# Expert weight tiles stored as 8192-byte rows, and a tile ring laid out anew in 4096 more SBUF columns

## The chip, the core and the metric

The kernel runs on one core of one Trainium2 chip. The metric is device time in microseconds (us) of one launch, the median over several runs. Everything is float32; the weights lie in HBM and are loaded in each launch.

## The reference

Two layers (DEPTH = 2) over 256 context tokens and 256 latent tokens of width 1024. Each layer runs three token mixers side by side (S5 state space, latent attention, windowed attention), merges them, and then runs a mixture of experts; only the latent stream is returned, so the second layer leaves the context out of its last steps. What matters here is the second half of a layer, the experts:

```python
N_EXPERTS = 16; EXPERT_FF = 1024; CAPACITY_FACTOR = 2

def expert_choice_ffn(h, lp):
    B, N, D = h.shape
    cap = CAPACITY_FACTOR * N // N_EXPERTS                 # 32 tokens for each expert
    aff = softmax(h @ lp['w_router'], axis=-1)
    g, idx = lax.top_k(aff.swapaxes(1, 2), cap)
    xs = jax.vmap(lambda hb, ib: hb[ib])(h, idx)
    a = jnp.einsum('becd,edf->becf', xs, lp['w_gate'])     # w_gate, w_up, w_down: (2, 16, 1024, 1024)
    u = jnp.einsum('becd,edf->becf', xs, lp['w_up'])
    y = jnp.einsum('becf,efd->becd', jax.nn.silu(a) * u, lp['w_down']) * g[..., None]
    return scatter_add(idx, y)

def trunk_layer(xc, xl, ...):
    hc, hl = modulate(xc, ...), modulate(xl, ...)          # adaLN
    yc, yl = token_mixer(hc, hl, ...)                      # three branches, gates, w_out
    xl = layer_norm(ALPHA * xl + mod_l[2] * yl, ln1)
    fl = expert_choice_ffn(modulate(xl, ...), lp)
    xl = layer_norm(ALPHA * xl + mod_l[5] * fl, ln2)       # and the same for xc in layer 0
    return xc, xl
```

All 16 experts of both layers are used whatever the routing does: 3 matrices of 4 MB for each expert, 201 MB for each layer.

## The kernel before

`Net.build` (near L1690) runs the layers in order. `layer` (L1735) has a mixer part, in which S5, attention and gates are interleaved by hand (`fill`, `tick`), an output projection (`out_proj`, L1352), the first layer norm with the router (`out_norm`, `scores`, `choose`), and `moe` (L1569). A scheduler places the instructions of all engines after that; only those marked with `keep_in_program_order` stay where they were written. All loads are issued by SyncE (SP) on one queue.

**The tile ring.** `expert_ring` (L1395) cuts each expert into 12 tiles of 1 MB: a tile is two blocks of 128 rows of one matrix (`kh` and `kh + 1`), on 128 partitions with 2048 columns each. So there are 192 tiles for each layer. Its `grow` adds buffers to the ring as the rest of the layer frees them, `issue` loads the next tiles into the buffers that are ready, and `weight(i)` hands tile i to TensorE and gives the buffers of the tiles before it back to the ring. A buffer carries a number: from that tile on it is not reused (192: reused to the end; 0: used once). The load of a tile is one line:

```python
i = self.load(ap, self.ins[nm][l, e].rearrange("(k p) (c n) -> p k c n", p=128, n=NF)[:, kh:kh + 2])
```

In HBM the matrix lies row by row, so a partition gets two runs of 1024 floats, 4096 bytes each, from rows 128 apart. `hold=True` in `grow` leaves issuing to `feed`, which `out_proj` calls at every second of its eight steps, so that weights of the projection and expert tiles share the queue.

**Where the buffers lie.** One SBUF tile of 23360 columns, `arena`, holds most data, at places written out by hand in `PLACES` (L1868): `E`, `F1` to `F5` are ring buffers of 2048 columns in the arena, `lngb1` the rows of the first layer norm, `m2` the adaLN gate, `mht` and `mxn` router data, `eth`, `eht`, `m5`, `rwt`, `cm`, `ys` the experts' small buffers. Other ring buffers are blocks that the mixer has done with (`big`, `extra`, `h`), half of `xs` once, and `more` in layer 1. In layer 0 the ring has 21 buffers, five of them used once; in layer 1 it has 22, two of them used once.

**What consumes a tile.** In `moe` expert e takes 8 tiles for gate and up (TensorE, output `sc`), then SiLU on ACT and VectorE (L1616 to L1618), four transposes (`tp`), and 4 tiles for down (output `mm`). After every fourth expert the results are scattered; the tokens of the first four experts are gathered at the start and those of the later groups after experts 3, 6 and 8 (`F`, `ad`). In layer 0 each token tile has 64 rows (both streams), in layer 1 it has 32. In experts 9 to 15 of layer 0 the S5 setup of layer 1 (`s5_setup`, L511) is woven in: its loads `s5_prm`, `s5_dk`, `s5_b`, `s5_c` (shown as `in_s_prm` and so on), its arithmetic on VectorE (L550), and transposes on TensorE.

Of the kernel before, what the change touches and what calls it, by code (L numbers as in the profile page):

```python
# [14 lines left out]
D = 1024  # L15
KT = 8
DEPTH = 2
N_EXP = 16
# [139 lines left out]
class Net:  # L158
# [1236 lines left out]
    def expert_ring(self, l):  # L1395

        NF = 512 if l == 0 else 256
        view = lambda t: t.rearrange("p (k c n) -> p k c n", k=2, n=NF)
        ready, once, tiles, at = [], {"single": 0}, {}, [0, 0]

        def grow(*where, blocks=(), single=(), hold=False):


            for w, until in where:
                name = f"F{len(once)}"
                once[name] = until
                ready.append((name, view(self.buf(name, 2048, at=w))))
            for block, until in blocks:
                for i in range(0, int(block.shape[1]), 2048):
                    name = f"block{len(once)}"  # L1410
                    once[name] = until
                    ready.append((name, view(block[:, i:i + 2048])))
            for block in single:
                ready.append(("single", view(block)))
            if not hold:
                issue(len(ready))

        def issue(n, behind=False):

            for _ in range(min(n, len(ready), 192 - at[0])):  # L1420
                e, r = divmod(at[0], 12)
                a, kh = self.part_of(e, r)
                nm = ("w_gate", "w_up", "w_down")[a]
                name, ap = tiles[at[0]] = ready.pop(0)
                i = self.load(ap, self.ins[nm][l, e].rearrange("(k p) (c n) -> p k c n", p=128, n=NF)[:, kh:kh + 2])
                if behind:
                    self.tc.keep_in_program_order(i)
                at[0] += 1

        def weight(i):  # L1430
            while at[1] < i:
                name, ap = tiles.pop(at[1])
                at[1] += 1
                if at[0] < once.get(name, 192):
                    ready.append((name, ap))
                elif name in self.A.live:
                    self.free(name)
            issue(len(ready))
            return tiles[i][1]

        return weight, grow, lambda: issue(1, True)

    def part_of(self, e, r):
# [246 lines left out]
    def build(self, layers=(0, 1), stop=None):  # L1690
        tc, nc = self.tc, self.nc
        self.dbg_out = {}
        self.fillq, self.adaq, self.debt, self.ada_debt = [], [], 0.0, 0.0
        with tc.tile_pool(name="main", bufs=1) as main, \
                tc.tile_pool(name="small", bufs=1) as small, \
                tc.tile_pool(name="ps", bufs=1, space=PSUM) as psum:
            self.small, self.psum, self.main = small, psum, main
            self.sc = main.tile([128, KT * 32], F32, name="silu_c")
            self.modT = [main.tile([128, 6, KT, 2], F32, name=f"modT{i}") for i in range(2)]
            k1 = main.tile([128, 4], F32, name="k1")  # L1700
            self.mhalf, self.econst, self.hpi, self.ones1 = [k1[:, i:i + 1] for i in range(4)]
            for ap, val in ((self.mhalf, -0.5), (self.econst, math.e), (self.hpi, math.pi / 2), (self.ones1, 1.0)):
                nc.vector.memset(ap, val)
            self.const = main.tile([128, NCONST], F32, name="const")
            arena = main.tile([128, self.ARENA_COLS], F32, name="arena")
            self.A = Arena(arena, self.ARENA_COLS)
            self.adaR, self.OH, self.ah, self.cd, self.back, self.norm, self.rw, self.rrow = {}, {}, {}, {}, {}, {}, {}, {}
            self.adarow = [self.buf(f"ada{i}", 512, low=True) for i in range(2)]
            x = {t: self.buf(f"x{t}", D, low=True) for t in range(4)}
            self.ada_start()  # L1710
            self.load(self.const[:, 0:128], self.ins["const"][:, 0:128])
            self.S, self.early, self.stats, self.T, self.feed = {}, [], {}, {}, lambda: None
            self.setup = self.s5_setup(layers[0], self.S, 16)
            next(self.setup)
            self.stg = self.rot("stg", 1024, 4, True)
            hb = [self.block(f"h{i}", F32) for i in range(2)]
            bufs = [hb[i // 2][:, 2048 * (i % 2):2048 * (i % 2) + 2048] for i in range(4)]
            bufs += [self.block(f"extra{i}", F32)[:, 0:2048] for i in range(2)] + [self.buf("wada", 2048, True)]
            for k, _ in enumerate(self.ada_group(layers[0], 0, bufs)):
                if k == 4:  # L1720
                    for t in range(4):
                        self.load(x[t], self.xin(t))
                if k in (7, 8):
                    kc = len(self.early)
                    self.early.append(self.wload(self.w_in(layers[0], 0, 512)[:, 2 * kc:2 * kc + 2], 2, 512))
            self.free("wada")
            for l in layers:
                self.layer(l, x, 1 if l == 0 and 1 in layers else None)
            for t in (2, 3):
                self.load(self.out[0, (t - 2) * 128:(t - 1) * 128], x[t])  # L1730
# [4 lines left out]
    def layer(self, l, x, nxt):  # L1735
        tc, nc = self.tc, self.nc
# [3 lines left out]
        with tc.tile_pool(name=f"parts{l}", bufs=1, reuse_waits="tile") as self.R:  # L1740
# [16 lines left out]
            mT = self.buf("mT", KT * N, True, 12416 if full else None).rearrange("p (k n) -> p k n", k=KT)  # L1757
# [25 lines left out]
            T = self.T = self.PLACES[l]  # L1783
# [23 lines left out]
            else:  # L1807
                mb = self.block("big0", F32R)
                m = self.out_split(mT, [mb[:, 0:2048], mb[:, 2048:4096]])
            self.free("mT")  # L1810
            self.slots = self.buf("slots", 256, at=T["slots"])
            gb = self.ln_rows(l, 1)
            wr = self.buf("wr", 128, True, T["wr"]).rearrange("p (k e) -> p k e", k=KT)
# [7 lines left out]
            m2 = {}  # L1821
# [15 lines left out]
        with tc.tile_pool(name=f"late{l}", bufs=1, reuse_waits="tile") as pool:  # L1837
# [10 lines left out]
            for s in ((1, 0) if full else (1,)):  # L1848
                self.out_norm(l, pts[s], x, s, gb)
                if s == 2 - NS:  # L1850
# [9 lines left out]
            self.T = {}  # L1860
            tts = (0, 1, 2, 3) if full else (2, 3)
            self.free(*[n for n in self.A.live if n[0] in "EF"])
            self.finish(l, x, pts, nxt is not None)

    ARENA_COLS = 23360
    BLOCKS = dict(h0=4096, h1=4096, big0=4096, big1=4096, big2=2048, extra0=2064, extra1=2064)

    PLACES = [dict(E=((21312, 172), (19264, 172)), raff=9216, wr=9344, rls=9472, rw=9600, rrow=10112, slots=10240, mxn=(10496, 11520, 12544, 13568),  # L1868
                   oh=14592, lngb1=15104, m2=17152, mht=8192, eth=4096, eht=4608, m5=5120, rwt=5632, ys=6144, cm=5888,
                   F1=((4096, 0), (6144, 0)), F2=((17152, 160),), F3=((15104, 160),), F4=((0, 0), (2048, 0)),  # L1870
                   F5=((8192, 192),)),
              dict(E0=(7168, 192), E1=(13312, 0), E2=((15360, 192), (9216, 192), (11264, 192)),
                   raff=19200, wr=18944, rls=19072, rw=19264, rrow=19520, slots=18688, mxn=(17408, 6144), oh=18432,
                   lngb1=2048, m2=3072, mht=20288, eth=13312, eht=13568, m5=13824, rwt=14080, ys=14336, cm=18944,
                   F1=((21312, 192),), F2=((4096, 192),), F3=((2048, 192),), F4=((0, 0),), F5=((19264, 192),))]
    NWC = 4

    FEED_OUT = [[0, 1] * 4, [0, 1] * 4]
# [4 lines left out]
def _prepare(inputs):  # L1883
    f = lambda n: np.ascontiguousarray(np.asarray(inputs[n]))
    a = {}
    for n in ("x", "ctx", "w_in", "s5_w_glu", "win_sink", "w_branch", "w_out", "ln1_g", "ln1_b",
              "ln2_g", "ln2_b", "w_router", "w_gate", "w_up", "w_down"):
        a[n] = f(n)
    c, cc = f("c").reshape(D), f("c_ctx").reshape(D)
    a["c2"] = np.stack([cc.reshape(KT, 128), c.reshape(KT, 128)], -1).transpose(1, 0, 2).reshape(128, KT * 2)  # L1890

# [33 lines left out]
def _program(arrays, dbg=None, layers=(0, 1), **tckw):  # L1925
    tckw.setdefault("schedule_with_timeline_sim", True)
    import concourse.bacc as bacc
    import concourse.tile as tile

    nc = bacc.Bacc("TRN2", target_bir_lowering=False, num_devices=1)  # L1930
    ins = {n: nc.dram_tensor("in_" + n, v.shape, mybir.dt.from_np(v.dtype), kind="ExternalInput").ap()
           for n, v in arrays.items()}
    out = nc.dram_tensor("out_0", (1, 256, D), F32, kind="ExternalOutput").ap()
    with tile.TileContext(nc, **tckw) as tc:
        net = Net(tc, ins, out, dbg)
        net.build(layers)
    return nc, net
# [9 lines left out]
```

## Time and profile before

| what | value |
|---|---|
| time, median of 3 runs | 2122.13 us (2119.47 to 2123.6) |
| the profiled execution | 2119.83 us, span 2118.1 us |
| TensorE busy | 1805.4 us (85%) |
| VectorE, ACT, GpSimd busy | 1046.0, 610.9, 452.7 us |
| DMA | 544.20 MB, mean 257 GB/s |
| TensorE clock granted, mean | 0.912 |

The span runs from the first to the last instruction; the execution's own time is 1.7 us longer. The profile cuts the span into 40 slices of about 53 us. TensorE's busy time is modelled from its pipeline, so a high share does not say that it sets the pace; the waits and the chain of work that ended last say that. The DMA figures of a slice tell how near the 16 DMA engines are to what they can move.

### The profile page before, as it was taken

The numbers are of one execution on the slowest core, as the hardware profiler recorded it, in microseconds if no ns is written. First come the engines' busy times: TensorE is split into PE (matmuls) and PEld (weight loads), VectorE is DVE, ScalarE is ACT, GpSimd is POOL, SyncE is SP. The second block draws the span as 40 slices with busy tenths as digits, with TensorE's granted clock in tenths as the row PEclk, the third lists the DMA queues.
The fourth block names the chain that finished last, engine by engine and source line by source line (L and its number), as shares of the span: only waits on it lengthen the run. The fifth ranks groups of instructions, "written<-read, shape, count | busy, mean of one in ns | idle before, by whom it ended". The sixth has DMA issues, their size and how long they took to land. (4 is left out here: it accounts for less than half of the span.)

```text
span 2118.1 us, 31735 instructions
## 1 busy us (share of the span) xinstructions
PE 1805.4 (85%) x12425; PEld 1121.1 (53%) x12425; DVE 1046.0 (49%) x2431; ACT 610.9 (29%) x1353; POOL 452.7 (21%) x590
## 2 busy tenths in 40 slices
PE   5999899999998799999799889789997856676765
PEld 3876666677776534434233278787875422232222
DVE  6767666656538622322563357977757311110102
ACT  2344253444434320101110155654553100000000
POOL 5735320011135100001442025630114000000000
PEclk8899999999999799999999989999998987676766
DMA  8236745522247699999999623341467799999996
GB/s 310 63 125 218 249 135 167 162 70 70 61 131 288 249 358 409 409 409 404 405 402 395 270 65 98 86 145 50 114 243 272 313 408 409 409 409 409 409 409 270
DMA packets 222165, 544.20 MB, mean 257 GB/s; under 512 B 18624, under 2 KB 101696, under 8 KB 221120
## 3 DMA queue, kind: packets, MB, share of 16 engines
q1 hardware_dynamic: 222016, 542.18, 69.4%
q8 instruction: 98, 1.61, 0.3%
q14 instruction: 51, 0.42, 0.1%
HBM read 541.09 MB, written 1.05 MB: 256 GB/s over the span
## 5 line engine op out<-in xcount | busy, mean ns | idle before, releaser
L243 PE MATMUL F<-h,wc 128*128 128x256 f32 (+1 forms) x1200 | 237.8, 350 | 10.9 <-ACT arena L1295 8.9
L404 ACT ACTIVATE wc<-arena 128x512 fp32r<-128x512 f32 (+2 forms) x280 | 169.9, 619 | 223.1 <-DMA arena<-in_w_in 44.7
L407 DVE TENSOR_TENSOR wc<-arena,wc 128x512 fp32r<-128x512 f32 (+2 forms) x205 | 164.0, 812 | 115.0 <-ACT wc L404 114.2
L243 PE MATMUL sc<-arena,xs 128*32 128x256 f32 (+1 forms) x1176 | 166.5, 524 | 59.9 <-DMA arena<-in_w_up 35.0
L243 PEld LDWEIGHTS F<-h,wc 128*128 128x128 f32 x1200 | 189.0, 196 | 42.2 <-ACT arena L1295 9.9
L246 PE MATMUL tp<-const,arena 128*128 128x128 f32 (+2 forms) x819 | 137.1, 293 | 70.1 <-DVE arena L1618 14.3
L1641 DVE TENSOR_TENSOR arena<-mm,arena 32x512 f32<-32x512 f32 (+1 forms) x128 | 70.9, 554 | 217.1 <-PE mm L243 215.5
L407 POOL TENSOR_TENSOR wc<-arena,wc 128x512 fp32r<-128x512 f32 (+2 forms) x75 | 98.0, 1306 | 369.2 <-ACT wc L404 296.1
L243 PE MATMUL mm<-arena 128*32 128x256 f32 (+5 forms) x1076 | 164.4, 461 | 13.5 <-DMA arena<-in_w_down 6.9
L246 PEld LDWEIGHTS tp<-const,arena 128*128 128x128 f32 (+2 forms) x819 | 97.2, 147 | 130.8 <-issue 40.9
L238 ACT ACTIVATE arena<-tp 128x512 f32<-128x512 f32 (+3 forms) x142 | 61.9, 462 | 331.4 <-PE tp L246 313.5
L260 POOL TENSOR_TENSOR lnq<-lnq,k 128x1 f32<-128x1 f32 x22 | 17.6, 802 | 594.4 <-DVE lnq L307 556.7
L243 PEld LDWEIGHTS sc<-arena,xs 128*32 128x32 f32 (+1 forms) x1176 | 53.6, 132 | 151.7 <-issue 75.0
L243 PE MATMUL sc<-h,xs 128*32 128x256 f32 (+1 forms) x760 | 116.1, 537 | 13.3 <-DMA h<-in_w_up 8.2
L243 PEld LDWEIGHTS mm<-arena 128*64 128x64 f32 (+2 forms) x1076 | 69.6, 137 | 85.6 <-issue 43.0
L1616 ACT ACTIVATE arena<-sc 128x512 f32<-128x512 f32 (+1 forms) x32 | 15.7, 491 | 336.0 <-PE sc L243 336.0
L243 PE MATMUL sc<-big,xs 128*32 128x256 f32 (+1 forms) x688 | 91.6, 522 | 22.7 <-DMA big<-in_w_gate 12.6
L1618 DVE TENSOR_TENSOR arena<-arena,sc 128x512 f32<-128x512 f32 (+1 forms) x32 | 17.7, 553 | 181.6 <-PE sc L243 181.4
L1617 DVE SCALAR_TENSOR_TENSOR arena<-arena,sc 128x512 f32<-128x512 f32 (+1 forms) x32 | 17.7, 555 | 172.1 <-ACT arena L1616 172.0
L243 PE MATMUL mm<-wc,h 128*128 128x512 f32 (+2 forms) x288 | 81.3, 408 | 9.5 <-ACT h L496 5.3
L243 PE MATMUL F<-extra,wc 128*128 128x256 f32 (+1 forms) x432 | 85.2, 341 | 3.2 <-DVE arena L1330 2.9
L550 DVE TENSOR_TENSOR arena<-arena 128x64 f32<-128x64 f32 (+2 forms) x300 | 81.0, 316 | 12.8 <-POOL arena L553 6.1
(344 smaller groups left out, 3210.4 us busy)
## 6 DMA issues: line engine op xcount, KB each, us to landing
arena<-in_w_gate SPq DMA_DIRECT2D x53, 1024.0 KB, 18.1
arena<-in_w_down SPq DMA_DIRECT2D x48, 1024.0 KB, 18.2
arena<-in_w_up SPq DMA_DIRECT2D x44, 1024.0 KB, 18.5
arena<-in_w_ada SPq DMA_DIRECT2D x82, 512.0 KB, 4.9
h<-in_w_down SPq DMA_DIRECT2D x41, 1024.0 KB, 18.2
h<-in_w_up SPq DMA_DIRECT2D x37, 1024.0 KB, 15.9
arena<-in_w_in SPq DMA_DIRECT2D x66, 512.0 KB, 4.0
big<-in_w_gate SPq DMA_DIRECT2D x30, 1024.0 KB, 18.5
```

Source lines behind the costliest of these rows:

```text
L238: self.nc.scalar.activation(out, in_, AF.Copy)
L243: return self.nc.tensor.matmul(out, lhsT, rhs, start=start, stop=stop, skip_group_check=True)
L246: self.nc.tensor.transpose(out, in_, self.c("idn")[:n, :n])
L260: self.nc.gpsimd.tensor_tensor(out, in_, e.to_broadcast(list(in_.shape)), op=OP.pow)
L404: nc.scalar.activation(hi, src, AF.Copy)
L407: eng.tensor_tensor(lo, src, hi.bitcast(F32), op=OP.subtract)
L550: tt = lambda o, a, b, op: v.tensor_tensor(o, a, b, op=op)
L1616: nc.scalar.activation(th, gu[0][:, :NF], AF.Tanh, scale=0.5)
L1617: v.scalar_tensor_tensor(th, th, 1.0, gu[0][:, :NF], op0=OP.add, op1=OP.mult)
L1618: v.tensor_tensor(th, th, gu[1][:, :NF], op=OP.mult)
L1641: v.tensor_tensor(YS[n][o:o + 32, c * NF:(c + 1) * NF], yp[r:r + 32, :NF], m5[r:r + 32], op=OP.mult)
```

## The change

Three things are changed. The host stores each tile as one contiguous block of 128 rows of 8192 bytes, in the order in which SBUF takes them, and the load reads one row for each partition. The program is built with a descriptor scratch of 64 bytes, and the arena gets 4096 columns (16 KB on each partition) more. `PLACES` is written anew: the new columns, called `late` until the projection, take the norm rows, the gate and the experts' small buffers, and ring buffers take what these leave.

```diff
-                i = self.load(ap, self.ins[nm][l, e].rearrange("(k p) (c n) -> p k c n", p=128, n=NF)[:, kh:kh + 2])
+                i = self.load(ap, self.ins[nm][l, e, kh // 2].rearrange("p (k c n) -> p k c n", k=2, n=NF))
...
+            self.buf("late", 4096, at=self.LATE)
             self.adarow = [self.buf(f"ada{i}", 512, low=True) for i in range(2)]
...
-            self.free("mT")
+            self.free("mT", "late")
+            grow(*T["E3"], hold=True)
             self.slots = self.buf("slots", 256, at=T["slots"])
...
             self.free(*[n for n in self.A.live if n[0] in "EF"])
+            self.buf("late", 4096, at=self.LATE)
             self.finish(l, x, pts, nxt is not None)
 
-    ARENA_COLS = 23360
+    ARENA_COLS = 27456
+    LATE = 23360
...
-    PLACES = [dict(E=((21312, 172), (19264, 172)), raff=9216, wr=9344, rls=9472, rw=9600, rrow=10112, slots=10240, mxn=(10496, 11520, 12544, 13568),
-                   oh=14592, lngb1=15104, m2=17152, mht=8192, eth=4096, eht=4608, m5=5120, rwt=5632, ys=6144, cm=5888,
-                   F1=((4096, 0), (6144, 0)), F2=((17152, 160),), F3=((15104, 160),), F4=((0, 0), (2048, 0)),
...
+    PLACES = [dict(E=((21312, 172), (19264, 172), (17152, 160)), E3=((15104, 160),), raff=9216, wr=9344, rls=9472, rw=9600,
+                   rrow=10112, slots=10240, mxn=(10496, 11520, 12544, 13568), oh=14592, lngb1=23360, m2=25408, mht=8192,
+                   eth=23360, eht=23872, m5=24384, rwt=24896, cm=25152, ys=25408,
+                   F1=((4096, 192), (6144, 192)), F2=(), F3=(), F4=((0, 0), (2048, 0)), F5=((8192, 192),)),
...
-                   lngb1=2048, m2=3072, mht=20288, eth=13312, eht=13568, m5=13824, rwt=14080, ys=14336, cm=18944,
-                   F1=((21312, 192),), F2=((4096, 192),), F3=((2048, 192),), F4=((0, 0),), F5=((19264, 192),))]
+              dict(E0=(7168, 192), E1=(13312, 192), E2=((15360, 192), (9216, 192), (11264, 192)),
+                   E3=((2048, 192), (5120, 192)),
...
+                   lngb1=23360, m2=24384, mht=20288, eth=23360, eht=23616, m5=23872, rwt=24128, ys=24384, cm=18944,
+                   F1=((21312, 192),), F2=((25408, 192),), F3=(), F4=((0, 0),), F5=((19264, 192),))]
...
+    for n in ("w_gate", "w_up", "w_down"):
+        a[n] = f(n).reshape(DEPTH, N_EXP, 4, 2, 128, D).swapaxes(3, 4).reshape(DEPTH, N_EXP, 4, 128, 2 * D)
...
-    nc = bacc.Bacc("TRN2", target_bir_lowering=False, num_devices=1)
+    nc = bacc.Bacc("TRN2", target_bir_lowering=False, num_devices=1, dynamic_dma_scratch_size=64)
```

The ring of layer 0 keeps 21 buffers, of which three instead of five are used once; that of layer 1 has 23, one used once.

The scheduler then gives another order. Three places on SP follow; a row is a load, out<-in and its shape, and x2 means two in a row. The first is the output projection of layer 0, before:

```order
L229 DMA arena<-in_w_gate 128x2x1024
L229 DMA arena<-in_w_out 128x1024 x2
L229 DMA arena<-in_w_up 128x2x1024
L229 DMA extra_5691<-in_w_down 128x2x1024
L229 DMA arena<-in_ctx 128x1024
L229 DMA extra_5690<-in_w_down 128x2x1024
L229 DMA arena<-in_x 128x1024
L229 DMA arena<-in_ln_g 128x1024
L229 DMA arena<-in_ln_b 128x1024
```

and with the change:

```order
L229 DMA arena<-in_w_gate 128x2048
L229 DMA arena<-in_w_out 128x1024 x2
L229 DMA arena<-in_w_up 128x2048
L229 DMA extra_5692<-in_w_gate 128x2048
L229 DMA arena<-in_ctx 128x1024
L229 DMA extra_5691<-in_w_down 128x2048
L229 DMA arena<-in_x 128x1024
L229 DMA arena<-in_w_down 128x2048
```

A tile's load has become one run of 2048 floats for each partition instead of two of 1024, and the rows of the layer norm (`in_ln_g`, `in_ln_b`) are gone from here: a tile stands in their place. They now stand near the start of the program, behind the first small loads and ahead of `w_in`:

```order
L229 DMA bglu<-in_s_bg 128x4
L229 DMA mlagn<-in_mla_gain 128x5
L229 DMA sink<-in_win_sink 128x8
L229 DMA arena<-in_ln_g 128x1024
L229 DMA arena<-in_ln_b 128x1024
L229 DMA arena<-in_w_in 128x2x512 x2
```

Those of layer 1 have moved likewise, from its output projection to ahead of the first loads of its mixer. The second place is in the experts of layer 0, where the loads of layer 1's S5 setup begin, before:

```order
L229 DMA arena<-in_s_b 128x2x64
L229 DMA arena<-in_w_up 128x2x1024
L229 DMA extra_5690<-in_w_up 128x2x1024
L229 DMA arena<-in_s_c 128x2x64 x2
L229 DMA extra_5691<-in_w_up 128x2x1024
L229 DMA h_5696<-in_w_down 128x2x1024
L229 DMA arena<-in_s_prm 128x96
L229 DMA arena<-in_s_dk 128x4
```

and with the change:

```order
L229 DMA arena<-in_s_b 128x2x64
L229 DMA arena<-in_w_up 128x2048
L229 DMA extra_5691<-in_w_down 128x2048
L229 DMA arena<-in_s_c 128x2x64 x2
L229 DMA arena<-in_s_prm 128x96
L229 DMA arena<-in_s_dk 128x4
```

The parameters `in_s_prm`, with which the setup's arithmetic begins, have two tiles instead of four between them and the first `in_s_b`. On TensorE the setup's transposes and small products stand where they stood: three transposes, four expert matmuls, one transpose and three more, as here with the change.

```order
L246 MATMUL tp_7253<-const,arena 128x128 x3
L243 MATMUL sc_7211<-arena,xs 64x512 x4
L246 MATMUL tp_7253<-const,arena 128x128
L246 MATMUL tp_7262<-const,arena 128x128 x3
L243 MATMUL sc_7211<-arena,xs 64x512 x4
```

The same five steps before the change had the same kinds and counts, and the fifth read its tile from `extra`.

## Rows read from the trace of the kernel before

**Rows 1.** Page, 40 slices: busy tenths of TensorE and DMA, and GB/s.
```profile
PE   5999899999998799999799889789997856676765
DMA  8236745522247699999999623341467799999996
GB/s 310 63 125 218 249 135 167 162 70 70 61 131 288 249 358 409 409 409 404 405 402 395 270 65 98 86 145 50 114 243 272 313 408 409 409 409 409 409 409 270
```
**Rows 2.** Chain that ended last, in order of time: start us, us, what.
```profile
1674.85 15.73 DMA big<-in_w_up
1690.58 20.38 DMA arena<-in_w_down
...
2079.79 19.09 DMA arena<-in_w_down
2098.87 0.04 issue
```
**Rows 3.** TensorE's waits, 1675 to 2100 us: waited for, us in total, times, longest.
```profile
PE sc L243 <- DMA arena<-in_w_up: 33.5, 18, 11.6
PE sc L243 <- DMA arena<-in_w_gate: 23.3, 18, 2.9
```
**Rows 4.** Windows: stretch, length, busy PE, PEld, DVE, ACT, POOL; clock, DMA share, GB/s.
```profile
800.00:950.00 150.00, 144.66 (x686) 58.06 (x682) 43.69 (x87) 13.56 (x28) 0.00 (x0) 1.00 1.03 409
1000.00:1150.00 150.00, 128.18 (x680) 45.92 (x682) 89.78 (x346) 23.26 (x83) 66.92 (x200) 0.97 1.03 400
1750.00:2050.00 300.00, 201.45 (x1980) 75.42 (x1972) 34.64 (x82) 10.24 (x26) 0.00 (x0) 0.72 1.03 409
```
**Rows 5.** Windows of the start, in which tiles of w_ada are loaded.
```profile
6.00:17.00 11.00, 7.08 (x60) 2.48 (x64) 4.13 (x30) 0.35 (x2) 8.77 (x2) 1.00 1.01 425
23.00:27.00 4.00, 0.29 (x4) 0.20 (x8) 4.00 (x11) 0.00 (x0) 1.62 (x2) 0.50 1.02 424
5.00:16.00 11.00, 6.08 (x52) 2.08 (x56) 3.17 (x22) 0.35 (x2) 9.77 (x2) 1.00 1.00 417
```
**Rows 6.** Page: DMA packets, and the instruction queues' among them.
```profile
DMA packets 222165, 544.20 MB, mean 257 GB/s; under 512 B 18624, under 2 KB 101696, under 8 KB 221120
...
q8 instruction: 98, 1.61, 0.3%
q14 instruction: 51, 0.42, 0.1%
```
**Rows 7.** TensorE's waits in the experts of layer 0, 740 to 1200 us.
```profile
PE tp L246 <- DVE arena L550: 10.3, 3, 6.1
...
PE sc L243 <- DMA arena<-in_w_up: 1.5, 1, 1.5
PE sc L243 <- DMA h<-in_w_up: 1.3, 2, 0.7
...
PE sc L243 <- DMA arena<-in_w_gate: 0.8, 2, 0.6
```
**Rows 8.** VectorE by line, 800 to 1200 us: count, busy us, mean ns, idle before.
```profile
L550 DVE TENSOR_TENSOR arena<-arena 128x64 f32<-128x64 f32 (+1 forms) x219 | 43.9, 248 | 3.9 <-POOL arena L553 1.4 <-DVE arena L550 0.2
...
L550 DVE TENSOR_TENSOR big<-arena 128x64 f32<-128x64 f32 x32 | 8.7, 271 | 0.9
```
**Rows 9.** Windows: behind the first loads, and the start of layer 1.
```profile
40.00:50.00 10.00, 9.82 (x37) 8.75 (x37) 10.00 (x17) 4.56 (x10) 8.00 (x10) 0.77 0.58 205
1200.00:1250.00 50.00, 36.40 (x127) 24.39 (x124) 36.70 (x80) 27.16 (x54) 13.48 (x13) 0.80 0.15 44
```
**Rows 10.** Page, DMA issues: count, KB each, median us from issue to landing.
```profile
arena<-in_w_gate SPq DMA_DIRECT2D x53, 1024.0 KB, 18.1
```

More of the change, by code (lines that the diff above doesn't have):

```diff
@@ L1862, in layer @@
             self.free(*[n for n in self.A.live if n[0] in "EF"])
+            self.buf("late", 4096, at=self.LATE)
             self.finish(l, x, pts, nxt is not None)
-    ARENA_COLS = 23360
+    ARENA_COLS = 27456
+    LATE = 23360
     BLOCKS = dict(h0=4096, h1=4096, big0=4096, big1=4096, big2=2048, extra0=2064, extra1=2064)
-    PLACES = [dict(E=((21312, 172), (19264, 172)), raff=9216, wr=9344, rls=9472, rw=9600, rrow=10112, slots=10240, mxn=(10496, 11520, 12544, 13568),
-                   oh=14592, lngb1=15104, m2=17152, mht=8192, eth=4096, eht=4608, m5=5120, rwt=5632, ys=6144, cm=5888,
-                   F1=((4096, 0), (6144, 0)), F2=((17152, 160),), F3=((15104, 160),), F4=((0, 0), (2048, 0)),
-                   F5=((8192, 192),)),
-              dict(E0=(7168, 192), E1=(13312, 0), E2=((15360, 192), (9216, 192), (11264, 192)),
-                   raff=19200, wr=18944, rls=19072, rw=19264, rrow=19520, slots=18688, mxn=(17408, 6144), oh=18432,
-                   lngb1=2048, m2=3072, mht=20288, eth=13312, eht=13568, m5=13824, rwt=14080, ys=14336, cm=18944,
-                   F1=((21312, 192),), F2=((4096, 192),), F3=((2048, 192),), F4=((0, 0),), F5=((19264, 192),))]
+    PLACES = [dict(E=((21312, 172), (19264, 172), (17152, 160)), E3=((15104, 160),), raff=9216, wr=9344, rls=9472, rw=9600,
[4 more added lines that the diff above has]
+                   E3=((2048, 192), (5120, 192)),
+                   raff=19200, wr=18944, rls=19072, rw=19264, rrow=19520, slots=18688, mxn=(17408, 4096), oh=18432,
+                   lngb1=23360, m2=24384, mht=20288, eth=23360, eht=23616, m5=23872, rwt=24128, ys=24384, cm=18944,
+                   F1=((21312, 192),), F2=((25408, 192),), F3=(), F4=((0, 0),), F5=((19264, 192),))]
     NWC = 4
@@ L1886, in _prepare @@
     for n in ("x", "ctx", "w_in", "s5_w_glu", "win_sink", "w_branch", "w_out", "ln1_g", "ln1_b",
-              "ln2_g", "ln2_b", "w_router", "w_gate", "w_up", "w_down"):
+              "ln2_g", "ln2_b", "w_router"):
         a[n] = f(n)
+    for n in ("w_gate", "w_up", "w_down"):
+        a[n] = f(n).reshape(DEPTH, N_EXP, 4, 2, 128, D).swapaxes(3, 4).reshape(DEPTH, N_EXP, 4, 128, 2 * D)
     c, cc = f("c").reshape(D), f("c_ctx").reshape(D)
```

## The prediction

> **What bounds the kernel now.** I read the page's slices first, then the chain of waits, then TensorE's waits in the two expert stages, then windows of the stages. The slices show two plateaus on which DMA moves about 409 GB/s: slices 16 to 22 (experts of layer 0) and 33 to 39 (experts of layer 1) [rows 1]. The mixers between them leave the queue half empty. A plateau of DMA is a bound only where somebody waits for it, and here the two stages differ.
>
> In layer 1 the chain runs through loads of expert tiles from 1674.85 us to the last landing at 2098.87 us, and then 19 us of scatter and norm [rows 2]. TensorE waits for tiles of gate and up throughout, 33.5 and 23.3 us in the two largest groups alone [rows 3]; it is busy in 201 of 300 us, while the queue never leaves 409 GB/s [rows 4]. So each 1 MB tile (1.0486 MB by its bytes) costs 1.0486 / 0.409 = 2.564 us, and the stage ends when the last tile is in.
>
> In layer 0 DMA is as full, but TensorE is nearly full as well: 144.7 of 150 us, later 128.2 of 150 [rows 4]. Its waits there are small: 10.3 us for the VectorE arithmetic of the next layer's S5 setup, and 1.5 + 1.3 + 0.8 = 3.6 us for tiles [rows 7]. Both are close to the bound, TensorE a little more so; what DMA gains there will be paid out only in part.
>
> **Longer rows, layer 1.** The change adds no work to any engine and takes none away; it halves the packets of a tile from 256 to 128. The kernel already loads tiles in that form: `w_ada` at the start comes as 1 MB tiles with 8192-byte rows, and seven of them make 896 packets. The packet counts show that such a row stays whole: 222165 - 221120 = 1045 packets are 8 KB or more, 149 of them belong to the instruction queues, and 896 remain [rows 6]. While those loads have the queue to themselves, it moves 425 and 424 GB/s, against 409 with 4096-byte rows [rows 5, 4]. At 425 a tile costs 2.467 us, 0.097 less. From the landing at 1690.58 us to the one at 2098.87 us there are 408.3 / 2.564 = 159 tiles [rows 2], so this term is 159 x 0.097 = **-15.4 us**. The start's stretches are short, so for the low end I take the window that includes the run-up, 417 GB/s [rows 5], which is 2.515 us and -7.8; I choose the upper one because two separate windows agree on it.
>
> The Trainium skill (DMA: Bandwidth & Descriptors, Why small descriptors are slow) gives a packet a fixed overhead of about 3 cycles, and its section on where 436 GB/s comes from a fabric of 850 MHz. With eight packets less on each of 16 engines that would be an estimated 28 ns for a tile and 4.5 us for the stage instead of 15.4. The two rates above show more than three times that, so I keep the measured pair.
>
> **One more buffer, layer 1.** The ring has 23 buffers instead of 22, and two of them (`E3`) are granted before the projection ends instead of after the norm. The queue has room then (243 to 313 GB/s in the slices before the plateau [rows 1]), so one tile more is in when the plateau begins: **-2.5 us**. The ends are 0, if the buffer comes free too late to be used, and -5.0 for two tiles.
>
> **Layer 0.** The ring keeps 21 buffers, two more of them for good. The 3.6 us of waits for tiles should go, since DMA gets 0.097 us ahead with each tile from 800 us on. The setup's parameters stand two tiles nearer to its first load in SP's order, so its VectorE arithmetic can begin 2 x 2.5 = 5 us earlier, out of a wait of 10.3 us. Sum **-8.6 us**. The lower end is 0, because TensorE is nearly full and can lose elsewhere what it saves here; the upper end is 3.6 + 10.3 = 13.9, all these waits.
>
> **What is moved.** The norm rows of layer 0 (two loads of 0.52 MB, some 2.6 us of queue) go from the projection to the start, ahead of `w_in`. I cost that at nothing: behind the first loads the queue falls to 58% [rows 9] while VectorE is full there, so it is VectorE that sets the pace; without that cover it is +2.6. The rows of layer 1 go ahead of the mixer's first `w_in` loads, where DMA is 15% busy [rows 9], cost 0, again +2.6 without cover. SP's queue holds seven tiles in flight (18.1 us from issue to landing, at 2.56 each [rows 10]); a shorter tile shortens that line for the small loads as well, by 0.7 us, which I don't count. The smaller scratch costs nothing: every load in the profile is issued by SP, none by GpSimd. The new places in the arena cost no instruction, only what waits for whom.
>
> **Sum.** -15.4 - 2.5 - 8.6 = -26.5 us. The profiled execution took 2119.83 us, which gives 2093.3; the median of the runs shown is 2.3 us above it, so I predict **2095.6 us**. Less than about 0.2% (4.2 us) can't be told from no change for this kernel.
>
> **Rivals.**
> - *TensorE keeps layer 0 as long as it was.* For it speaks that it is busy 96% of the first 150 us [rows 4] and that its program is the same; against it, that 13.9 us of waits have a cause that moves. Then 2095.6 + 8.6 = 2104.2.
> - *The plateau doesn't move*, because something other than the packets holds 409 GB/s, or because the longer row is cut again on its way. For it: it stands at 409 for 300 us without a flicker [rows 4], like a limit. Against it: 425 and 424 on the same queue [rows 5], and rows that stay whole [rows 6]. Then 2095.6 + 15.4 = 2111. The Trainium skill has a rule of this kind (DMA: Bandwidth & Descriptors, Where 436 GB/s comes from): for loads from HBM the HBM side binds at some 358 GB/s, whatever the packets. The trace disagrees, since both rates lie above it.
> - *Slower: the S5 setup is late in layer 0.* TensorE takes its instructions in order, and the setup's transposes stand among the experts' matmuls. VectorE spends 43.9 + 8.7 = 52.6 us on the setup [rows 8], of which TensorE waits for 10.3. The new order of loads could bring an `s5_b` or `s5_c` piece late, and then TensorE stands, tiles aren't released and the queue stops as well. If all 52.6 us were exposed: 2095.6 + 8.6 + 42.3 = 2146. It decides once that wait passes 10.3 + 15.4 + 2.5 = 28 us. Against it: the transposes stand at the same places in TensorE's order, and the parameters come sooner, not later.
> - *The change doesn't do what it says*: if buffers come free no sooner and rows are cut, nothing is left, 2122.
>
> **How the numbers follow.** I give the forecast 0.72, TensorE keeping layer 0 0.12, the plateau that doesn't move 0.08, the late setup 0.04, no effect 0.04. The first three are faster than 0.2%, so 0.92 faster, 0.04 the same, 0.04 slower. For the range, the forecast's own unknowns reach from all upper ends (-15.4 - 5.0 - 13.9 = -34.3, or 2087.8) to its low rate (2095.6 + 7.6 = 2103.2); the first rival lies at 2104.2 and the second at 2111. A range from 2088 to 2112 holds these three; outside are the two last cases and some of the forecast's own tails.
>
> **What would show it.** Right: DMA at 420 to 426 GB/s on the plateau of layer 1, some 173,000 packets, issue to landing near 17.5 us, the chain in that stage still through tiles and some 16 us shorter, TensorE's waits for tiles in layer 0 gone, and layer 1 starting 5 to 12 us earlier. Wrong in the largest term: a plateau still at 409. Wrong in the third: the gap between the two plateaus starts where it did. Wrong altogether: a wait of TensorE for L550 of over 28 us, or TensorE instead of DMA at the end of the chain in layer 1.

## The result, and the profile after

The changed kernel takes 2098.97 us (median, 2095.9 to 2101.72), the kernel before 2121.56 us in the same session: a ratio of 0.9893, 95% interval 0.9875 to 0.9912, or 22.6 us less. The profiled execution has a span of 2095.6 us, 22.5 less than before.

The page's slices and packets, to be held against [rows 1] and [rows 6]:

```profile
DMA  9236744522247689999999733342267799999996
GB/s 334 67 123 218 245 144 163 163 78 71 60 132 274 248 354 421 421 421 416 416 413 351 297 91 94 81 129 63 76 214 297 291 420 421 421 421 421 420 421 272
DMA packets 173013, 544.20 MB, mean 260 GB/s; under 512 B 18624, under 2 KB 101696, under 8 KB 122816
```

Both plateaus stand at 421 instead of 409 GB/s, with 49152 packets fewer, and none of the 8192-byte rows is cut: 173013 - 122816 = 50197 packets are 8 KB or more, which are the 1045 of before and 384 x 128 = 49152 new ones. The windows say the same (length, busy PE, PEld, DVE, ACT, POOL, granted clock, DMA share, GB/s), where [rows 4, 5] had 425, 424, 409 and 409:

```profile
6.00:17.00 11.00, 6.47 (x64) 2.28 (x64) 4.01 (x29) 0.35 (x2) 8.89 (x2) 1.00 1.01 421
23.00:27.00 4.00, 0.19 (x4) 0.19 (x8) 4.00 (x11) 0.00 (x0) 1.61 (x2) 0.50 1.01 428
800.00:950.00 150.00, 145.42 (x687) 56.36 (x684) 42.59 (x86) 13.65 (x28) 0.00 (x0) 1.00 1.01 421
...
1750.00:2050.00 300.00, 196.70 (x2008) 73.78 (x2000) 35.86 (x84) 10.15 (x26) 0.00 (x0) 0.74 1.01 421
```

The two windows of the start load the same bytes by the same code as before; they now read 421 and 428. So such short stretches tell a rate only to within a few GB/s, while 421 holds for 300 us.

The chain that ended last (start us, us, what) still goes through tiles to the last landing, now at 2056.33 + 19.66 = 2076.0 us instead of 2098.9 [rows 2]; each step is about 19.8 us, eight tiles of 2.49:

```profile
1660.63 13.67 DMA arena<-in_w_down
1674.37 20.12 DMA extra<-in_w_gate
...
2056.33 19.66 DMA arena<-in_w_down
2076.04 1.98 PE mm L243 x16
```

TensorE still waits for tiles there, 1675 to 2080 us (us in total, times, longest); the two largest groups were 33.5 and 23.3 us [rows 3]:

```profile
PE sc L243 <- DMA arena<-in_w_up: 20.1, 19, 6.3
PE mm L243 <- DMA arena<-in_w_down: 13.4, 14, 1.7
PE sc L243 <- DMA h<-in_w_gate: 13.2, 9, 5.6
```

In the experts of layer 0, 740 to 1200 us, no tile is among the large waits any more, but the wait for the setup's arithmetic (L550) is as long as it was, 9.4 + 0.9 + 0.7 = 11.0 us against 10.3 in [rows 7]:

```profile
PE tp L246 <- DVE arena L550: 9.4, 3, 7.1
PE tp L246 <- DVE arena L1618: 5.2, 7, 0.9
PE mm L243 <- ACT arena L238: 4.9, 7, 0.7
...
PE tp L246 <- DVE big L550: 0.9, 1, 0.9
PE sc L243 <- DVE big L550: 0.7, 1, 0.7
```

The difference of 22.5 us, cut at four points of the timeline: TensorE's first expert matmul of layer 0, its first matmul on the last tile of layer 0, its first expert matmul of layer 1, and the last landing.

| stretch | before | after | difference |
|---|---|---|---|
| start to the experts of layer 0 | 733.0 | 731.1 | -1.9 |
| experts of layer 0 | 469.2 | 461.3 | -7.9 |
| from there to the experts of layer 1 (its mixer) | 449.8 | 453.0 | +3.2 |
| tiles of layer 1, to the last landing | 446.9 | 430.6 | -16.3 |
| end | 19.2 | 19.6 | +0.4 |

### The profile page after: what moved, and what is told of

The parts are those of the page before. It is cut to its first block, busy times and chain, and to the rows that moved or that the text cites. A ratio compares the mean times of both kernels' runs of the same rounds, so it can differ in the third digit from the quotient of the medians.

```text
span 2095.6 us, 31733 instructions
## 1 busy us (share of the span) xinstructions
PE 1791.9 (86%) x12425; PEld 1112.2 (53%) x12425; DVE 1042.9 (50%) x2431; ACT 611.3 (29%) x1353; POOL 451.5 (22%) x590
## 2 busy tenths in 40 slices
DMA packets 173013, 544.20 MB, mean 260 GB/s; under 512 B 18624, under 2 KB 101696, under 8 KB 122816
## 3 DMA queue, kind: packets, MB, share of 16 engines
HBM read 541.09 MB, written 1.05 MB: 259 GB/s over the span
## 4 chain that ended last, share of the span: by engine, by line
PE 54%; DMA 23%; DVE 14%; POOL 3%; ACT 3%; issue 3%; SPq 0%; POOLq 0%; ACTq 0%; DVEq 0%
PE sc L243 16%; PE mm L243 16%; PE F L243 13%; DMA arena<-in_w_down 4%; DMA arena<-in_w_up 4%; PE tp L246 4%; PE ad L243 4%; DMA arena<-in_w_gate 3%; DVE extra L852 2%; DVE wc L407 2%; DMA h<-in_w_gate 2%; DMA big<-in_w_gate 2%; DMA arena<-in_w_in 1%; DMA extra<-in_w_up 1%; DMA extra<-in_w_gate 1%
## 5 line engine op out<-in xcount | busy, mean ns | idle before, releaser
L243 PE MATMUL sc<-arena,xs 128*32 128x256 f32 (+1 forms) x1336 | 188.5, 522 | 33.7 <-DMA arena<-in_w_up 20.5
L243 PE MATMUL mm<-arena 128*32 128x256 f32 (+5 forms) x1244 | 186.1, 467 | 21.9 <-DMA arena<-in_w_down 13.4
L246 PE MATMUL tp<-const,arena 128*128 128x128 f32 (+2 forms) x819 | 137.5, 293 | 70.4 <-DVE arena L1618 11.6
L1641 DVE TENSOR_TENSOR arena<-mm,arena 32x512 f32<-32x512 f32 (+1 forms) x128 | 70.9, 554 | 219.0 <-PE mm L243 217.4
L238 ACT ACTIVATE arena<-tp 128x512 f32<-128x512 f32 (+3 forms) x142 | 61.9, 463 | 341.7 <-PE tp L246 297.4
L243 PEld LDWEIGHTS sc<-arena,xs 128*32 128x32 f32 (+1 forms) x1336 | 60.8, 131 | 139.7 <-issue 68.7
L243 PEld LDWEIGHTS mm<-arena 128*32 128x32 f32 (+2 forms) x1244 | 76.3, 137 | 107.2 <-issue 50.5
L1618 DVE TENSOR_TENSOR arena<-arena,sc 128x512 f32<-128x512 f32 (+1 forms) x32 | 17.7, 554 | 178.2 <-PE sc L243 177.9
L243 PE MATMUL sc<-big,xs 128*32 128x256 f32 (+1 forms) x632 | 80.8, 487 | 25.2 <-DMA big<-in_w_gate 13.0
L243 PEld LDWEIGHTS sc<-h,xs 128*32 128x32 f32 (+1 forms) x752 | 36.8, 133 | 89.2 <-issue 60.7
## 6 DMA issues: line engine op xcount, KB each, us to landing
arena<-in_w_down SPq DMA_DIRECT2D x61, 1024.0 KB, 19.8
arena<-in_w_gate SPq DMA_DIRECT2D x48, 1024.0 KB, 19.7
big<-in_w_up SPq DMA_DIRECT2D x26, 1024.0 KB, 19.8
```

What stands on the lines that cost most here:

```text
L238: self.nc.scalar.activation(out, in_, AF.Copy)
L243: return self.nc.tensor.matmul(out, lhsT, rhs, start=start, stop=stop, skip_group_check=True)
L246: self.nc.tensor.transpose(out, in_, self.c("idn")[:n, :n])
L1618: v.tensor_tensor(th, th, gu[1][:, :NF], op=OP.mult)
L1641: v.tensor_tensor(YS[n][o:o + 32, c * NF:(c + 1) * NF], yp[r:r + 32, :NF], m5[r:r + 32], op=OP.mult)
```

## The experiments

All are compared with runs of the kernel before on the same chip. The stretches are those of the table above (experts 0, mixer 1, tiles 1), each from one profiled execution; the ratio is to the kernel before, with its 95% interval. Where an expectation speaks of the experts of layer 1 "to the end", it counts to the end of the program and from some 4 us later than the table: its 446.1 us for the changed kernel are 430.6 + 19.6 = 450.2 by the table's points.

| run | median us | ratio | experts 0 | mixer 1 | tiles 1 | plateau GB/s |
|---|---|---|---|---|---|---|
| before | | | 469.2 | 449.8 | 446.9 | 409 |
| after | 2098.97 | 0.9893 [0.9875, 0.9912] | 461.3 | 453.0 | 430.6 | 421 |
| e1_rows_only | 2111.44 | 0.9943 [0.9924, 0.9962] | 470.0 | 451.7 | 434.4 | 421 |
| e2_space_only | 2114.72 | 0.9959 [0.9943, 0.9974] | 463.5 | 453.8 | 442.4 | 410 |
| e3_rows_2048 | 2163.78 | 1.0191 [1.0168, 1.0214] | 485.1 | 455.5 | 468.5 | 389 |
| e4_norm_rows_late | 2104.41 | 0.9911 [0.9888, 0.9935] | 460.3 | 454.2 | 432.2 | 421 |
| e7_scratch_only | 2120.62 | 0.9991 [0.9978, 1.0003] | 470.6 | 450.9 | 445.9 | 410 |
| e8_one_buffer_fewer | 2102.6 | 0.9905 [0.9886, 0.9924] | 460.7 | 454.3 | 434.5 | 421 |
| e9_buffers_used_once | 2104.22 | 0.9913 [0.9882, 0.9943] | 466.7 | 454.3 | 430.7 | 421 |
| e10_rows_16k | 2100.23 | 0.9891 [0.9871, 0.9912] | 460.6 | 454.4 | 429.4 | 423 |
| e11_after_again | 2100.43 | 0.9896 [0.9872, 0.992] | 460.9 | 453.3 | 430.6 | 421 |
| e12_rows_16k_again | 2095.23 | 0.9871 [0.9845, 0.9897] | 460.9 | 453.2 | 428.6 | 423 |

### Only the rows, only the places

e1 is the kernel before with the load of 8192-byte rows and the host's layout, all places as before:

```diff
-                i = self.load(ap, self.ins[nm][l, e].rearrange("(k p) (c n) -> p k c n", p=128, n=NF)[:, kh:kh + 2])
+                i = self.load(ap, self.ins[nm][l, e, kh // 2].rearrange("p (k c n) -> p k c n", k=2, n=NF))
...
```

> The kernel before with nothing but the 8192-byte rows; arena, ring and order of instructions stay. If the shorter tile is the main term (theory): plateau of layer 1 at 421 GB/s as in the changed kernel, 159 tiles x 0.073 us = -11.6 us there, and 2 to 4 us in layer 0 where TensorE waited 3.6 us for tiles, so about 2107 us. If the new places of the buffers made the gain (rival): 2121 us.

e2 is the other half, the changed kernel with that line and the host's layout as before the change.

> The changed kernel with the old rows of 4096 bytes; arena, ring and order as in the changed kernel. Theory: plateau at 409 GB/s, one buffer more in layer 1 (-2.5 us) and some 4 us in layer 0, so 2114 to 2117 us. Rival, space as the main cause: about 2099 us.

e2's 2114.72 us lie where they were expected; e1's 2111.44 are 4 more than expected, and the 2 to 4 us of layer 0 did not come. In layer 1 the two changes nearly add up. The rows alone give 446.9 - 434.4 = 12.5 us, the places alone 446.9 - 442.4 = 4.5, together 16.3. The plateau is the rows' doing alone; windows of e1 and of e2:

```profile
1750.00:2050.00 300.00, 204.08 (x2040) 78.98 (x2040) 36.16 (x86) 11.62 (x29) 0.00 (x0) 0.74 1.01 421
```
```profile
1750.00:2050.00 300.00, 205.44 (x1979) 76.82 (x1980) 34.19 (x80) 10.14 (x26) 0.00 (x0) 0.69 1.03 410
```

In layer 0 they don't. The rows alone change nothing (470.0 against 469.2 us): the queue reaches 421 GB/s and then stands below it, and TensorE still waits 3.8 us for tiles. SP waits for buffers there: from 1040 to 1160 us its waits for TensorE's gate and up matmuls are 60.1 us and those for its down matmuls 29.2, and from 1100 to 1140 us three loads are in flight on average, against seven from 800 to 950 us. The changed kernel's queue falls below 421 there as well (355 GB/s from 1130 to 1150 us), yet TensorE waits only 0.4 us for tiles in it. Windows of e1:

```profile
1100.00:1120.00 20.00, 18.79 (x113) 6.96 (x115) 12.54 (x56) 3.34 (x14) 10.97 (x38) 1.00 0.91 328
1120.00:1140.00 20.00, 16.76 (x84) 6.21 (x80) 12.92 (x35) 2.21 (x8) 10.77 (x35) 1.00 0.94 352
```

The places alone give 5.7 us there, and only with them are the rows worth another 2.2 (463.5 against 461.3).

### Shorter rows

e3 is the changed kernel with four rows of 2048 bytes for each partition in place of one of 8192, so that the same places get twice the packets of before.

```diff
-                i = self.load(ap, self.ins[nm][l, e, kh // 2].rearrange("p (k c n) -> p k c n", k=2, n=NF))
+                i = self.load(ap.rearrange("p k c n -> p (k c n)").rearrange("p (q n) -> p q n", q=4), self.ins[nm][l, e, kh // 2].rearrange("q p n -> p q n"))
...
```

The host's layout changes with it, and a tile stays one contiguous block.

> The changed kernel with tiles of 2048-byte rows, four for each partition; the 1 MB block stays contiguous in HBM and the order stays. If each packet costs a fixed time (theory): 8 x (a + 8192 b) = 2.491 us and 16 x (a + 4096 b) = 2.564 us give a = 9 ns and b = 0.0369 ns a byte, so 32 x (a + 2048 b) = 2.71 us for a tile, 387 GB/s on the plateau, and 159 x 0.22 = 35 us more in layer 1, with layer 0 now also behind DMA by some 20 us: 2135 to 2155 us. If the contiguous block in HBM is what helps (rival): 421 GB/s and 2099 us.

It is slower than before, with the plateau at 389 GB/s in the window, as the fixed cost says; so the contiguous block is not what helps. The whole, 2163.78 us, is 9 us above the expected range: of the 66.7 us between the two profiles 37.9 lie in the tiles of layer 1 (35 expected) and 23.8 in the experts of layer 0 (some 20 expected), and 2.5 each in the start and the mixer were not expected.

```profile
1800.00:2050.00 250.00, 167.50 (x1548) 61.81 (x1552) 28.72 (x67) 8.22 (x21) 0.00 (x0) 0.67 1.05 389
```

At 389, 409 and 421 GB/s a tile costs 2.696 us with 512 packets, 2.564 with 256, 2.491 with 128. Each of the 16 DMA engines handles 32, 16 or 8 of them, so the steps are 0.132 / 16 = 8.2 ns and 0.073 / 8 = 9.1 ns for each packet less: nearly a fixed cost. The packets' own records agree. In these plateaus they last 88, 164 and 314 ns on average for 2048, 4096 and 8192 bytes, so two short ones take some 13 ns more than one of twice the length. With a DMA share of 1.05, 1.03 and 1.01 the records cover the engines all the time, and overlap a little, which accounts for 13 instead of 8 to 9 ns.

### The norm rows

e4 is the changed kernel with the loads of the first norm's rows kept at the place where they are written, as before the change; the scheduler then also orders some of the other engines' work otherwise.

```diff
-        self.load(gb[:, 0], self.ins[f"ln{n}_g"][l][None, :].to_broadcast([128, D]))
-        self.load(gb[:, 1], self.ins[f"ln{n}_b"][l][None, :].to_broadcast([128, D]))
+        for i, m in enumerate("gb"):
+            d = self.load(gb[:, i], self.ins[f"ln{n}_{m}"][l][None, :].to_broadcast([128, D]))
+            if n == 1:
+                self.tc.keep_in_program_order(d)
```

> The changed kernel with the norm rows' loads kept where the program writes them, that is in the projections again. In the changed kernel layer 1's mixer took 3.2 us longer than before. If the early norm rows cause that (theory 1): about 2096 us. If it is the scheduler's new order of TensorE and ACT in the mixer (theory 2): the first layer's start is the same or up to 2 us slower, and the mixer moves by some us to either side, as this kernel is scheduled anew too: 2095 to 2103 us, and the norm rows' place in the trace has no wait of w_in behind it.

The mixer of layer 1 takes 454.2 us, no less than with the rows ahead of it (453.0), and the start 736.2 us against 731.1. So neither is seen to lose by the norm rows' early loads. The median, 2104.41 us, lies above what both theories expected, but its interval overlaps the changed kernel's.

### The scratch alone

e7 is the kernel before with the descriptor scratch of 64 bytes.

> The kernel before with the descriptor scratch of 64 bytes and nothing else. Theory 1 (the scratch does nothing but free SBUF): no change, 0.999 to 1.001 of the kernel before, plateaus at 409 GB/s. Theory 2 (a part of the 0.9893 is the scratch's own): 0.996 to 0.998, with a plateau or a gap that moves though rows and places stand as before.

No change: the interval holds 1, and the slices read as in [rows 1] to within a few GB/s on the plateaus (409 or 410). It is also a second sample of the old order: its stretches differ from those of before by 1.4, 1.1 and 1.0 us.

### One buffer less in layer 1

```diff
-                   E3=((2048, 192), (5120, 192)),
+                   E3=((2048, 192),),
```

> The changed kernel without one buffer (5120) of layer 1's ring, 22 instead of 23. Theory 1 (each buffer that is there before the plateau begins is worth one tile at the plateau's rate): the stage from the first tile's use in layer 1 to the end takes 446.1 + 2.5 = 448.6 us, the whole 2101.5. Theory 2 (the buffer comes free too late, and the 4.4 us that the new places gave in layer 1 come from the order of the loads): 446 us and 2099.

Theory 1: 434.5 us of tiles against 430.6, with 21 tiles landed when the experts begin, as before the change, instead of 22. The 3.9 us are more than one tile of 2.49. They arise at the beginning of the stage: counted from TensorE's first matmul of the experts, the 24th tile lands at 11.6 us instead of 8.9, the 28th at 22.7 instead of 18.8, and from the 40th on both kernels take 2.51 us for each tile. What the other 1.4 us are isn't settled.

### Buffers used once in layer 0

```diff
-                   F1=((4096, 192), (6144, 192)), F2=(), F3=(), F4=((0, 0), (2048, 0)), F5=((8192, 192),)),
+                   F1=((4096, 0), (6144, 0)), F2=(), F3=(), F4=((0, 0), (2048, 0)), F5=((8192, 192),)),
```

> The changed kernel with the two buffers F1 of layer 0 used once, as before the change, so that its ring has two buffers fewer to the end; the rest of the places and the new order stay. Theory 1 (the 6 to 8 us in the experts of layer 0 come from the buffers that are kept): the stage from first use to the last tile goes back from 461 to 467 to 470 us, TensorE waits for tiles there again, the whole 2105 to 2108. Theory 2 (they come from the S5 setup's earlier parameters): the stage stays at 460 to 463 us, the whole 2098 to 2101.

466.7 us and 2104.22, each just below theory 1's lower bound, with tile waits back: 7.6 us in the stretch, 5.6 of them in three waits for one block (TensorE's waits, 731 to 1197.7 us):

```profile
PE tp L246 <- DVE arena L1618: 6.9, 9, 0.9
PE sc L243 <- DMA h<-in_w_up: 5.6, 3, 4.0
```

But it is no clean test. The scheduler put the S5 setup 200 us earlier (its parameters are issued at 773.0 us instead of 975.1), and L550 is no longer among TensorE's waits at all. So what the kept buffers give is shown only with the setup elsewhere. The early setup didn't make the stretch short either: its sum of waits, 24.7 us, is lower than the changed kernel's 26.3, yet the stretch is 5.4 us longer. Around the longest tile wait TensorE's granted clock is lower, as two windows show:

```profile
1130.00:1150.00 20.00, 16.03 (x52) 7.59 (x50) 1.86 (x3) 0.60 (x1) 0.00 (x0) 0.69 0.95 385
1150.00:1160.00 10.00, 10.00 (x34) 4.19 (x36) 0.00 (x0) 0.60 (x1) 0.00 (x0) 0.76 0.55 206
```

The changed kernel has 1.00 in both windows. Within them e9 has 0.50 from 1139 to 1150 us, the lower of the two levels (1.2 GHz), and 1.00 (2.4 GHz) again from 1157 us on; TensorE had stood for 3.97 us before a matmul at 1139.18 us.

### Still longer rows

e10 fills neighbouring buffers of layer 1 in pairs, by one load of 2 MB with rows of 16384 bytes, for 66 of its tiles; e12 is the same kernel again, next to the changed kernel (e11).

```diff
+                src = self.ins[nm][l, e, kh // 4]
...
+                    b = ready.pop(two)
+                    c = ready.pop(next(j for j, x in enumerate(ready) if x[0] == mate[b[0]][0]))
+                    self.load(mate[b[0]][1], src)
+                    tiles[at[0]], tiles[at[0] + 1] = b, c
...
-        a[n] = f(n).reshape(DEPTH, N_EXP, 4, 2, 128, D).swapaxes(3, 4).reshape(DEPTH, N_EXP, 4, 128, 2 * D)
+        a[n] = f(n).reshape(DEPTH, N_EXP, 4, 2, 128, D).reshape(DEPTH, N_EXP, 2, 4, 128, D).swapaxes(3, 4).reshape(DEPTH, N_EXP, 2, 128, 4 * D)
```

> The changed kernel with layer 1's neighbouring buffers filled in pairs, by one load of 2 MB with rows of 16384 bytes (the host stores the tiles in pairs). Theory 1 (a packet has a fixed cost of some 9 ns, as 388, 409 and 421 GB/s at 2048, 4096 and 8192 bytes fit): such a pair moves at some 427 GB/s, 2.454 us for each MB tile instead of 2.491, and with some 66 tiles in pairs layer 1 ends 2.4 us sooner, the whole 2096.5. Theory 2 (rows are cut at 8192 bytes, or 421 is another limit than the packets): the plateau stays at 421 and the whole at 2099, or 1 to 5 us more, since a pair has to wait until both of its buffers are free.

> The changed kernel once more, beside the next kernel on the same chip, and as a second sample of the stages. Both theories: 0.988 to 0.991 of the kernel before. The experts of layer 0 take 460 to 462 us, the mixer of layer 1 453 to 455.5 us (449.8 to 451.7 in the three profiles with the old order), the experts of layer 1 to the end 445.5 to 448.5 us, if these differences belong to the program; if a stage differs by more than 2 us from the first profile, that stage's figure is a matter of the single execution.

> The kernel with pairs of tiles in rows of 16384 bytes once more, beside the changed kernel. Theory 1 (a fixed cost of some 9 ns for each packet): plateau 423 to 424 GB/s again, the experts of layer 1 to the end 442 to 444 us, and the whole 2 to 4 us (0.1 to 0.2%) below the changed kernel's median. Theory 2 (the rate rises, but pairs wait for their second buffer and the end is no sooner): 446 us or more in that stage, and a median within 1 us of the changed kernel's or above it.

The plateau rises as the fixed cost says: with some 35% of the plateau's bytes in rows of 16384 a tile comes to 2.478 us on average, or 423 GB/s. Page of e10:

```profile
GB/s 334 67 123 207 220 171 151 162 93 60 71 111 281 272 337 421 422 422 416 416 414 348 317 84 101 81 122 71 54 220 279 288 423 425 423 423 423 422 423 297
```

In its layer 0 every tile is still loaded alone, and its 128 rows of 8192 bytes lie 16384 bytes apart in HBM; the plateau there reads 421 and 422 all the same, so the rows need not lie end to end. The tiles of layer 1 take 1.2 and 2.0 us less than in the changed kernel, of 2.4 expected. In time the medians are 2100.23 and 2095.23 against 2098.97 and 2100.43: the intervals overlap, so a gain over the changed kernel isn't shown, neither the 2096.5 us expected of e10 nor the 2 to 4 us expected of e12. e11 repeats the changed kernel's stretches within 0.4 us.

## Why the prediction was right, point by point

The forecast was 26.5 us less, in a range from 10 to 34; it came out at 22.6. The largest term was right in its mechanism. But it was too large, the second was too small, most of the reason for the third failed, and one cost was missing; that the sum is so near is in part luck, as these errors partly cancel.

- **Longer rows, layer 1 (-15.4): right in kind, too large.** e1 gives -12.5, and after against e2 430.6 - 442.4 = -11.8. The step that failed is the rate: "I choose the upper one because two separate windows agree on it". Those windows were 11 and 4 us long. At 421 GB/s a tile takes 2.491 us, and 159 x 0.073 = 11.6 us, close to what was measured. The low end, 417 GB/s, was as near as the chosen value.
- **The cost of a packet.** The runs show 8.2 to 9.1 ns for a packet. The Trainium skill (DMA: Bandwidth & Descriptors, Why small descriptors are slow) has about 3 cycles, which was 28 ns for a tile by the prediction's estimate; the trace has 73. The Trainium skill (DMA: Bandwidth & Descriptors, Where 436 GB/s comes from) has the HBM side bind at some 358 GB/s; here one core reads 421 for 300 us.
- **One more buffer, layer 1 (-2.5): right in kind, too small.** e2 gives -4.5, after against e1 -3.8, and taking that buffer away costs 3.9 (e8). With the first term the stage is 16.3 us shorter, against 17.9 forecast.
- **Layer 0 (-8.6): the size was right by luck, most of the reason was not.** The stage is 7.9 us shorter. Of the forecast, 3.6 us were tile waits, and these are gone (0.4 left). The other 5 were "its VectorE arithmetic can begin 2 x 2.5 = 5 us earlier", and that failed: TensorE's wait for L550 went from 10.3 to 11.0 us. [rows 8] already held a bound: VectorE stood 1.4 us in all before L550 for GpSimd's L553, the first step on the parameters. The timelines show the rest. Before (start us, us, engine, line; in brackets idle time and what ended it):

```profile
999.98 0.69 DVE L1618 TENSOR_TENSOR arena<-arena,sc 128x512 f32<-128x512 f32 x1 [5.55 <-PE sc L243]
1000.59 0.51 DVE L550 TENSOR_TENSOR arena<-arena 128x32 f32<-128x32 f32 x3
1002.91 0.19 DVE L550 TENSOR_TENSOR arena<-arena 128x32 f32<-128x32 f32 x1 [1.42 <-POOL arena L553]
...
997.45 5.43 POOL L553 TENSOR_TENSOR arena<-k,arena 128x32 f32<-128x32 f32 x1 [282.89 <-DMA arena<-in_s_prm]
```

and after:

```profile
997.73 0.69 DVE L1618 TENSOR_TENSOR arena<-arena,sc 128x512 f32<-128x512 f32 x1 [5.55 <-PE sc L243]
998.34 0.51 DVE L550 TENSOR_TENSOR arena<-arena 128x32 f32<-128x32 f32 x3
...
984.79 5.43 POOL L553 TENSOR_TENSOR arena<-k,arena 128x32 f32<-128x32 f32 x1 [272.22 <-DMA arena<-in_s_prm]
```

  The parameters arrived 12.7 us sooner and GpSimd (L553) took them up at once. VectorE's first L550 stands behind the experts' own product (L1618) in its order, which waits for TensorE's matmuls; it began 2.3 us sooner, and the stage itself had begun 1.9 us sooner. The wait of 1.42 us for L553 is gone, but the long part of the setup stands behind the experts' next product (L1641), which VectorE began at 1009.26 us before and at 1007.01 after, again 2.3 us sooner. What bounded the setup was VectorE's order, not the load. Over the stretch TensorE's waits fell from 31.0 to 26.3 us: tiles -3.2, L1618 and L1666 -2.8, L550 and L238 +1.7, others -0.4. Of the other 3.2 of the 7.9 us, 1.6 lie in TensorE's modelled busy time (437.3 to 435.7) and 1.3 in one idle stretch before an `sc` matmul that the profile puts down to "issue" (no wait that it shows) and that the changed kernel lacks. By e1 and e2 the gain needs the places; which buffer gives what isn't settled, since e9 moved the setup too.
- **What is moved (0): right for what was listed.** The norm rows cost nothing (e4), the scratch nothing (e7), and the start varies between profiles of kernels with the same loads there, from 733.0 to 737.6 us with the old order and from 730.8 to 736.8 with the new, so its -1.9 can't be put down to the change.
- **Missing: the mixer of layer 1, +3.2.** Three profiles with the old order (before, e1, e7) have 449.8 to 451.7 us there, the nine of the changed kernel and of the experiments built on it 453.0 to 455.5. Neither rows nor scratch do that, and e4 shows that the norm rows don't. What is left is the order that the new places led the scheduler to, or the places themselves; which step of it costs the time was not found. One wait of TensorE is new, 2.5 us for the attention's L1041 on VectorE, in seven of the nine; but e4 has 0.2 us of it and e9 none, and their mixers (454.2 and 454.3 us) are no shorter.
- **What would show it.** 173,000 packets and 421 GB/s came as said, the chain through tiles 16.3 us shorter as well. Layer 1 began 6.7 us earlier, in the range of 5 to 12, by a layer 0 of -7.9, a start of -1.9 and a mixer of +3.2; without the start, which isn't shown to be the change's, it would be just below that range. The 17.5 us from issue to landing did not come, because the loads in flight became eight instead of seven (last section): the page has 19.7 where [rows 10] had 18.1.

```profile
arena<-in_w_gate SPq DMA_DIRECT2D x48, 1024.0 KB, 19.7
```

- **The rivals.** The slower one, a late setup, asked for a wait for L550 of over 28 us; it is 11. The plateau that doesn't move is excluded by the 421 GB/s of the changed kernel and of e1, TensorE keeping layer 0 as long as it was by the 461.3 us (469.2 before), no effect by the interval. The one on layer 0 would have been right for the rows alone (e1).

## What to carry to other kernels

Where a queue is full and somebody waits for it, fewer and longer packets are worth a nearly fixed time for each packet saved, here 8 to 9 ns on each of the 16 engines. Take the rate from a long stretch, since the windows of 11 and 4 us were off by a third of the gain. A faster queue is paid out only where buffers are free to receive it: here the rows alone gave 12.5 us in layer 1 but nothing in layer 0. Before a load is counted as "sooner", look at what stands ahead of its first user in that user's own order.

## What was not expected

With 8192-byte rows SP is no longer held while it issues a load. SP's timeline on the plateau before (start us, us):

```profile
1799.11 2.30 SPq L229 DMA_DIRECT2D big<-in_w_down  x1
1801.51 2.32 SPq L229 DMA_DIRECT2D extra<-in_w_down  x1
```

and after:

```profile
1800.09 0.33 SPq L229 DMA_DIRECT2D big<-in_w_up  x1
1802.57 0.33 SPq L229 DMA_DIRECT2D extra<-in_w_up  x1
```

Before, an issue lasted nearly as long as a tile, and 18.7 us from issue to landing are 7.3 tiles of 2.564; now it takes 0.33 us, and 19.8 us are eight tiles of 2.49. With 2048-byte rows (e3) an issue lasts 2.53 us, and from issue to landing it is 14.4 us, or 5.3 tiles of 2.70. So more loads are in flight as their packets get fewer.

Is it then the issuing that sets the rate? Where the queue isn't full, the same load of 256 packets is issued in 0.46 us, here before the plateau of layer 1 in the kernel before:

```profile
1556.84 0.46 SPq L229 DMA_DIRECT2D h<-in_w_gate  x1
```

One of 512 packets took 0.50 us in e3 at the corresponding place. So the issue itself is short, and the 2.3 us on the plateau are SP held by a full queue. Eight, on the other hand, is the program's own limit: its loads use eight landing semaphores in turn, and in the changed kernel each of the 119 issues from 1750 to 2050 us comes within 0.2 us behind the landing of the eighth load before it, against 13% of them before. Nor do more bytes in flight make the queue faster by themselves: e10 has eight loads in flight, many of them of 2 MB, which take 23 to 30 us to land, and its plateau is the 423 GB/s that the packets' cost gives. No run changes the number of loads in flight alone, so that it adds nothing to the rate is argued and not shown.
